# Twelve matrix products of zeros at the start of a hybrid decoder block on one core

## Chip, core and metric

The kernel runs on one NeuronCore of a Trainium2 chip. The metric is the device time of one execution in microseconds. The names of the engines are those of the profile: PE is TensorE (PEld its weight loads), DVE is VectorE, ACT is ScalarE, POOL is GpSimd and SP is SyncE, which issues most DMA transfers.

## The reference

The kernel computes one decoder block for a sequence of 1024 tokens of width 1024, all in float32: a gated recurrence of 8 heads beside a causal pooling mixer, then a squared-ReLU MLP of width 4096, each followed by a scaled residual and a layer norm.

```python
proj = x @ w_in                       # 1024 x 7168
q, f_pre, i_val, o_gate, pool_v, gate_a, gate_b = split(proj)
a = rms_norm_per_head(hgrn2(silu(q), 1 - f, i_val, log(f))) * g * sigmoid(o_gate) @ w_a
b = (causal_mean(pool_v) - pool_v) @ w_pool * pool_scale
mix = (sigmoid(gate_a) * a + sigmoid(gate_b) * b) @ w_out
x = layer_norm(alpha * x + mix)
x = layer_norm(alpha * x + square(relu(x @ w_up)) @ w_down)
```

## The kernel before

**Products.** A float32 matrix is split in two parts: ScalarE casts it to a rounded high part (L111 for weights, L116 for activations) and VectorE subtracts that from the source to get the low part (L112, L117). A product is then three matmuls (L188, L189, L190 in `prod`: high by high, high by low, low by high). The large products go through a seven-product Strassen scheme over halves of the tokens, the inner dimension and the columns. `pair` builds the steps for one pair of column blocks, `run` issues them, `w_blocks` loads four weight quarters, and the sums and differences of weight quarters are made on VectorE (L227, L262, L266).

**The start.** `prm_r` (lower bound logits, norm gain, pool scale) is loaded in three transfers from ScalarE's queue (L361 to L363), transposed on TensorE (L366), copied (L367), and made into `lb` and `one_lb` by VectorE and one exponential (L372 to L379). SyncE issues the loads of x in half rows (`load_x`, L386), mixed with loads of w_in quarters (L209): first the left half of token tiles 0 to 3 with the left quarters of the first block, then their right half with those of the second block, then token tiles 4 to 7, then the remaining quarters. Each tile of x is 128 tokens; `transposed_parts` (L147) turns four 128x128 squares of it into one PSUM bank and `split_into` makes the two parts, so that the tokens stand on the free axis. `first_tokens` does this for the quarters a11 and a12 of x (token tiles 0 to 3). `row_sums` then forms the Strassen sums of x on VectorE in place (L165 to L170), `second_tokens` transposes those, and `run_second` issues the remaining products.

**After that.** For each of the eight heads: products for its inputs, the recurrence in chunks (`hgrn`), and between them the pooling and gate products. Then the output products, the first layer norm, and the MLP with hidden blocks passed through DRAM.

**What sets the order.** The program is written once, and a scheduler that simulates a timeline orders the instructions of each engine (`schedule_with_timeline_sim`); on the chip each engine takes its instructions in that order. PSUM has eight banks: four of tag `pj`, two of `hg` and two of `tr`. The transposes of L147 take turns on the two `tr` banks, so a group of four waits until the group before the last has been read by VectorE's subtraction (L117). SBUF pools are filled from two sides; `const` holds the identity matrix for transposes, a mask and small constants.

Of the kernel before, what the change touches and what calls it, by code (L numbers as in the profile page):

```python
# [9 lines left out]
F32 = mybir.dt.float32  # L10
# [6 lines left out]
P = 128  # L17
# [12 lines left out]
PRIO_LAST = 3000  # L30
QUARTER = HALF // 2
PRIO = 60
WINDOWS = (2, 4, 8, 16)
ALPHA = 2.0 ** 0.25
LN_EPS = 1e-5
# [6 lines left out]
def tile_hybrid_block(  # L42
# [19 lines left out]
    V, A, G, PE = nc.vector, nc.scalar, nc.gpsimd, nc.tensor  # L62
# [5 lines left out]
    const = ctx.enter_context(tc.tile_pool(name="const", bufs=1))  # L68
# [10 lines left out]
    def nm(s):  # L79
        seq[0] += 1  # L80
        return f"{s}_{seq[0]}"
# [5 lines left out]
    def ps_tile(tag="pj", bufs=4):  # L87
        return pp.tile([P, HALF], F32, tag=tag, name=nm("ps_" + tag), bufs=bufs)
# [28 lines left out]
        V.tensor_sub(t[:, 1], src, f(t[:, 0]))  # L117


    ident = const.tile([P, P], F32, name="ident")  # L120
    make_identity(nc, ident)
    cmask = const.tile([P, P], F32, name="cmask")
# [61 lines left out]
    def prod(ps, w, name, first):  # L184
        wh, wl = w
        for k in range(CH):
            th, tl = xp[name][k][:, 0], xp[name][k][:, 1]
            PE.matmul(ps, wh[:, k], th, start=first and k == 0, stop=False, skip_group_check=True)  # L188
            PE.matmul(ps, wh[:, k], tl, start=False, stop=False, skip_group_check=True)  # L189
            PE.matmul(ps, wl[:, k], th, start=False, stop=k == CH - 1, skip_group_check=True)  # L190
# [51 lines left out]
    def pair(raw, rooms, takes, pz_tag="pj", twin=False):  # L242
# [5 lines left out]
        def copied(room, ps):  # L248
            t = room()
            A.copy(t, ps)  # L250
            return t

        def added(t, ps):
            V.tensor_add(t, t, ps)  # L254
            return t
# [25 lines left out]
        def p7(w):  # L281
            ps["z"] = ps_tile(pz_tag, 4 if pz_tag == "pj" else 2)
            prod(ps["z"], w, "s3", True)
            with tc.high_priority(PRIO):
                takes[0](added(c[11], ps["c"]))
                c[22] = copied(rooms[2], ps["z"])

        def p6(w):
            prod(ps["a"], w, "s2", False)
            with tc.high_priority(PRIO):  # L290
                c[21] = copied(rooms[1], ps["a"])

        def p4(w):
            prod(ps["z"], w, "a22", False)
            with tc.high_priority(PRIO):
                takes[2](added(c[21], ps["z"]))

        def p5(w):
            prod(ps["a"], w, "s1", False)
            with tc.high_priority(PRIO):  # L300
                takes[3](added(c[22], ps["a"]))

        def p3(w):
            prod(ps["a"], w, "s4", False)
            with tc.high_priority(PRIO):
                takes[1](ps["a"])
# [52 lines left out]
    with tc.tile_pool(name="xr", bufs=8, side="right", reuse_waits="tile") as xr:  # L359
# [5 lines left out]
        ps = ps_tile("tr", 2)  # L365
# [101 lines left out]
    with tc.tile_pool(name="tmp", bufs=1, side="right", reuse_waits="tile") as tmp:  # L467
# [79 lines left out]
        def pooled(g):  # L547

            j, win = 2 * g, WINDOWS[g]

# [239 lines left out]
    with tc.tile_pool(name="mg", bufs=1, side="right", reuse_waits="tile") as mg:  # L790
# [5 lines left out]
        for u in range(2):  # L796
            for jh in range(2):
# [8 lines left out]
                for g in (2 * jh, 2 * jh + 1):  # L806
# [6 lines left out]
                    for i in range(2):  # L813
                        w = slice(i * P, (i + 1) * P)
                        ps = ps_tile("hg", 2)
# [98 lines left out]
    with tc.tile_pool(name="up", bufs=1, side="right", reuse_waits="tile") as up:  # L914
# [85 lines left out]
        def add_to(t, n, ps):  # L1000
            y = r[t][:, n * HALF : (n + 1) * HALF]
            if (t, n) not in touched:
                V.scalar_tensor_tensor(y, y, ALPHA, ps, ALU.mult, ALU.add)
                touched.add((t, n))
            else:
                V.tensor_add(y, y, ps)
# [38 lines left out]
        def down_tile(ops, chain, fresh, c):  # L1045
            ps = banks[1 - chain][c]
            w = slice(c * P, (c + 1) * P)
            for n in range(M):
                hh, hl, wh, wl = (t[:, n % 2] for t in ops[n // 2])
                PE.matmul(ps, hh[:, w], wh, start=fresh and n == 0, stop=False, skip_group_check=True)  # L1050
                PE.matmul(ps, hh[:, w], wl, start=False, stop=False, skip_group_check=True)  # L1051
                PE.matmul(ps, hl[:, w], wh, start=False, stop=n == M - 1, skip_group_check=True)  # L1052
            return ps
# [74 lines left out]
    for i, c in ((0, 0), (0, 1), (1, 0), (0, 2), (1, 1), (1, 2), (0, 3), (1, 3)):  # L1128
        _, _, chain, fresh, (_, nh) = ends[i]
        ps = down_tile(ops[i], chain, fresh, c)  # L1130
        with tc.high_priority(PRIO) if c == CH - 1 else nullcontext():
            add_to(c, nh, ps)
# [36 lines left out]
```

## Time and profile before

| | us |
|---|---|
| median of three runs | 1501.65 |
| lowest and highest of them | 1501.17, 1505.73 |
| the profiled execution | 1503.59 |
| its span, first to last instruction | 1501.8 |
| PE busy | 1473.9 |
| DVE busy | 1117.6 |
| ACT busy | 743.4 |
| POOL busy | 53.5 |

The profiled execution is one more run, with the profiler on; its span leaves out 1.8 us around the instructions. Its instructions carry their start from the beginning of the span. A row of the timeline gives start, duration, engine, line, operation, result and sources, shapes and a count where equal neighbours are merged; in brackets stands how long the engine had been idle, and what ended it. TensorE's rows overlap, as its matmuls are pipelined; the distance of two starts is what one costs. The transposes of L147 and the product of L690 are float32 operations, those of L188 to L190 run on the rounded parts.

### The profile page before, as it was taken

To read this page: it belongs to the slowest core of one execution; us is meant where nothing else is said; L and a number is where in the kernel's file an instruction comes from. 1 tells how busy PE (TensorE), PEld (TensorE's weight loads), DVE (VectorE), ACT (ScalarE), POOL (GpSimd) and SP (SyncE) were. 2 spreads that over 40 slices of the span, in tenths; PEclk is the share of its full clock that TensorE was granted. 3 is DMA by queue.
4 is the path that set the end of the run, shared out by engine and by line. 5 is a ranking of instruction groups with operands and counts; after the bars stand their busy time and mean duration, and the time that the engine had idled before them with its cause. 6 is when DMAs were issued, how large, how long until landed. Compare 5 with 4: busy or idle time off the path is not lost.

```text
span 1501.8 us, 19944 instructions
## 1 busy us (share of the span) xinstructions
PE 1473.9 (98%) x7201; PEld 1222.7 (81%) x7201; DVE 1117.6 (74%) x1789; ACT 743.4 (49%) x1361; POOL 53.5 (4%) x244
## 2 busy tenths in 40 slices
PE   7999999999999999999999999999999999999997
PEld 5788888888888888888788877888888888888886
DVE  7778888989867777566766786666666787777977
ACT  4655555565564656554333245555555544333435
POOL 0000000000000000000001200000000100000000
PEclk9999999999999999999999999999999999999999
DMA  5112222222222122378654134444455783544422
GB/s 169 43 43 71 68 66 64 78 71 65 90 64 70 57 78 85 109 239 262 208 171 165 61 100 151 150 154 155 155 192 201 252 292 122 175 134 169 140 71 112
DMA packets 141825, 192.15 MB, mean 128 GB/s; under 512 B 9344, under 2 KB 80032, under 8 KB 141728
## 3 DMA queue, kind: packets, MB, share of 16 engines
q1 hardware_dynamic: 139792, 184.32, 37.1%
q0 software_dynamic: 1152, 4.19, 0.7%
q10 hardware_dynamic: 784, 2.38, 0.4%
q8 instruction: 56, 0.92, 0.3%
q14 instruction: 41, 0.34, 0.1%
HBM read 136.86 MB, written 54.00 MB: 127 GB/s over the span
## 4 chain that ended last, share of the span: by engine, by line
PE 91%; DVE 4%; DMA 3%; issue 1%; ACT 0%; SPq 0%; DVEq 0%; ACTq 0%
PE ps_pj L188 16%; PE ps_pj L190 16%; PE ps_pj L189 16%; PE ps_pj L1052 4%; PE ps_pj L1051 4%; PE ps_pj L1050 4%; PE ps_pj L461 3%; PE ps_hg L190 2%; PE ps_hg L189 2%; PE ps_hg L188 2%; PE ps_pj L99 2%; PE ps_pj L100 2%; PE ps_pj L98 2%; PE ps_hg L1052 1%; PE ps_hg L1051 1%; PE ps_hg L1050 1%
## 5 line engine op out<-in xcount | busy, mean ns | idle before, releaser
L189 PE MATMUL ps_pj<-act,w 128*128 128x512 f32 x1088 | 428.4, 394 | 0.7 <-DVE act L117 0.7
L188 PE MATMUL ps_pj<-act,w 128*128 128x512 f32 x1088 | 424.2, 395 | 1.9 <-ACT act L116 1.0
L190 PE MATMUL ps_pj<-act,w 128*128 128x512 f32 x1088 | 419.2, 392 | 0.4 <-DVE w L112 0.4
L188 PEld LDWEIGHTS ps_pj<-act,w 128*128 128x128 f32 x1088 | 204.4, 188 | 45.2 <-ACT w L111 2.4
L190 PEld LDWEIGHTS ps_pj<-act,w 128*128 128x128 f32 x1088 | 204.8, 188 | 42.9 <-DVE w L112 1.9
L189 PEld LDWEIGHTS ps_pj<-act,w 128*128 128x128 f32 x1088 | 204.9, 188 | 41.7 <-DVE act L117 1.2
L111 ACT CAST w<-t 128x512 fp32r<-128x512 f32 x176 | 108.6, 622 | 157.7 <-PE ps_pj L189 95.1
L112 DVE TENSOR_TENSOR w<-raw,w 128x512 fp32r<-128x512 f32 x161 | 110.3, 688 | 100.0 <-ACT w L111 83.0
L111 ACT CAST w<-raw 128x512 fp32r<-128x512 f32 x161 | 99.3, 620 | 115.3 <-PE ps_pj L189 50.9
L112 DVE TENSOR_TENSOR w<-t,w 128x512 fp32r<-128x512 f32 x176 | 120.3, 687 | 29.7 <-ACT w L111 22.5
L1012 ACT CAST act<-act 128x1024 fp32r<-128x1024 f32 x66 | 67.0, 1051 | 110.5 <-issue 35.0
L461 PE MATMUL ps_pj<-act,w 128*128 128x512 f32 x384 | 90.6, 394 | 2.9 <-DVE ga L822 2.9
L1013 DVE TENSOR_TENSOR act<-act,act 128x1024 fp32r<-128x1024 f32 x66 | 79.5, 1221 | 18.5 <-ACT act L1012 18.5
L254 DVE TENSOR_TENSOR c<-c,ps_pj 128x512 f32<-128x512 f32 x95 | 64.7, 682 | 38.0 <-PE ps_pj L190 31.9
L1052 PE MATMUL ps_pj<-act,act 128*128 128x512 f32 x240 | 92.9, 389 | 0.0
L1051 PE MATMUL ps_pj<-act,act 128*128 128x512 f32 x240 | 92.9, 389 | 0.0
L1050 PE MATMUL ps_pj<-act,act 128*128 128x512 f32 x240 | 92.5, 389 | 0.0
L461 PEld LDWEIGHTS ps_pj<-act,w 128*128 128x128 f32 x384 | 73.1, 191 | 18.7 <-DVE ga L822 3.3
L250 ACT COPY c<-ps_pj 128x512 f32<-128x512 f32 x95 | 55.1, 582 | 10.6 <-PE ps_pj L190 10.3
L189 PE MATMUL ps_hg<-act,w 128*128 128x512 f32 x144 | 57.0, 396 | 0.0
L190 PE MATMUL ps_hg<-act,w 128*128 128x512 f32 x144 | 56.2, 390 | 0.0
L188 PE MATMUL ps_hg<-act,w 128*128 128x512 f32 x144 | 55.2, 391 | 0.0
(312 smaller groups left out, 2522.2 us busy)
## 6 DMA issues: line engine op xcount, KB each, us to landing
h<-c SPq DMA_DIRECT2D x105, 256.0 KB, 2.7
raw<-in_w_in_dram SPq DMA_DIRECT2D x96, 256.0 KB, 3.4
act<-h SPq DMA_DIRECT2D x78, 256.0 KB, 3.0
draw<-in_w_down_dram SPq DMA_DIRECT2D x16, 1024.0 KB, 7.9
raw<-in_w_up_dram SPq DMA_DIRECT2D x30, 512.0 KB, 4.2
hf<-h SPq DMA_DIRECT2D x34, 256.0 KB, 3.0
raw<-in_w_a_dram SPq DMA_DIRECT2D x16, 512.0 KB, 5.2
xr<-in_x_dram SPq DMA_DIRECT2D x16, 256.0 KB, 5.6
```

The lines of the kernel that those rows point to most:

```text
L111: A.copy(hi, src)
L112: V.tensor_sub(lo, src, f(hi))
L188: PE.matmul(ps, wh[:, k], th, start=first and k == 0, stop=False, skip_group_check=True)
L189: PE.matmul(ps, wh[:, k], tl, start=False, stop=False, skip_group_check=True)
L190: PE.matmul(ps, wl[:, k], th, start=False, stop=k == CH - 1, skip_group_check=True)
L254: V.tensor_add(t, t, ps)
L461: PE.matmul(banks[j], a[:, w], b, start=k == 0 and i == 0, stop=k == KT - 1 and i == 2, skip_group_check=True,)
L1012: A.copy(hi, src)
L1013: V.tensor_sub(lo, src, f(hi))
L1050: PE.matmul(ps, hh[:, w], wh, start=fresh and n == 0, stop=False, skip_group_check=True)
L1051: PE.matmul(ps, hh[:, w], wl, start=False, stop=False, skip_group_check=True)
L1052: PE.matmul(ps, hl[:, w], wh, start=False, stop=n == M - 1, skip_group_check=True)
```

## The change

Ahead of the other constants, a 128x128 tile of zeros is made in `const` by VectorE, a `tr` bank of PSUM is taken, and twelve products of that tile with itself are written into its first 128 columns, one over the other. Nothing reads them. The constant `IDLE_PRODUCTS` sets their number. The lines of the kernel move down, those above it by one and those below it by seven (L111 becomes L112, L147 becomes L154), and the `tr` banks of all later transposes change places. The scheduler orders the changed program anew.

```diff
+IDLE_PRODUCTS = 12
...
+    zeros = const.tile([P, P], F32, name="zeros")
+    V.memset(zeros, 0.0)
+    ps = ps_tile("tr", 2)
+    for _ in range(IDLE_PRODUCTS):
+        PE.matmul(ps[:, :P], zeros, zeros, start=True, stop=True)
     ident = const.tile([P, P], F32, name="ident")
     make_identity(nc, ident)
```

## Prediction before the run

> **What bounds the kernel now.** I read the page first, then the chain that ended last in order of time, then the first 55 us of the timeline engine by engine, since the change adds work only there.
>
> ```profile
> span 1501.8 us, 19944 instructions
> PE 1473.9 (98%) x7201; PEld 1222.7 (81%) x7201; DVE 1117.6 (74%) x1789; ACT 743.4 (49%) x1361; POOL 53.5 (4%) x244
> ...
> PE 91%; DVE 4%; DMA 3%; issue 1%; ACT 0%; SPq 0%; DVEq 0%; ACTq 0%
> ```
>
> The kernel is bound by TensorE: 98% busy, 91% of the chain. What remains of the chain lies mostly at the start. In order of time it begins:
>
> ```profile
> 3.78 6.04 DMA xr<-in_x_dram
> 9.83 4.79 DMA xr<-in_x_dram
> 14.67 0.41 DVE c L165
> ...
> 33.38 0.61 DVE act L117
> 34.04 0.66 PE ps_tr L147 x4
> 34.69 0.23 PE ps_hg L189
> ```
>
> The reader is to see three legs: to 14.6 us the chain is the arrival of x, from 14.67 to 34.0 us it is VectorE, and TensorE carries it only from 34.04 us. So TensorE time won before 34 us counts only where it lets VectorE's row of work end sooner. The windows say the same (stretch, length, then busy time and count of PE, PEld, DVE, ACT, POOL, granted clock, DMA share, GB/s):
>
> ```profile
> 0.00:8.55 8.55, 2.47 (x9) 1.69 (x9) 1.31 (x8) 1.82 (x3) 1.75 (x27) 1.00 0.66 205
> 8.55:11.97 3.42, 2.54 (x7) 1.86 (x8) 1.89 (x3) 1.86 (x4) 0.00 (x0) 1.00 1.06 366
> 11.97:15.38 3.41, 3.41 (x11) 2.62 (x10) 2.62 (x5) 2.15 (x4) 0.00 (x0) 1.00 1.09 365
> 15.38:34.00 18.62, 15.43 (x83) 12.08 (x81) 18.62 (x32) 7.54 (x14) 0.00 (x0) 1.00 0.37 112
> 715.00:722.00 7.00, 4.15 (x12) 2.95 (x11) 6.72 (x11) 2.39 (x5) 0.00 (x0) 0.76 0.81 286
> ```
>
> VectorE is busy for all 18.62 us from 15.38 to 34.00, while before that it has gaps and DMA is full.
>
> **Is the clock low at the start?** The granted clock reads 1.00 there, but durations contradict it:
>
> ```profile
> 4.66 0.71 PE L147 MATMUL ps_tr<-ident,xr 128*128 128x128 f32 x2
> 6.83 1.54 PE L147 MATMUL ps_tr<-ident,xr 128*128 128x128 f32 x6 [1.46 <-DMA xr<-in_x_dram]
> 15.40 0.60 PE L147 MATMUL ps_tr<-ident,xr 128*128 128x128 f32 x4
> 19.97 1.03 PE L147 MATMUL ps_tr<-ident,xr 128*128 128x128 f32 x8
> ```
>
> Two transposes take 0.71 us and six 1.54, so one more costs 0.21; later four take 0.60 and eight 1.03, so one more costs 0.11. Up to about 15.4 us TensorE runs at half speed. The window 715 to 722 shows a granted 0.76: 0.24 of 7 us lost, which is one stretch of 3.4 us at half clock, costing 1.7 us.
>
> **The change, part by part.**
>
> 1. *The zeros.* One fill of 128x128 on VectorE. No row of before has it; the nearest are GpSimd's fill of the same shape and a small operation of VectorE:
>
> ```profile
> 0.86 0.20 POOL masks.py:197 MEMSET ident<- 128x128 f32 x1
> 5.92 0.20 DVE L377 RECIPROCAL lb<-lb 128x8 f32<-128x8 f32 x1
> ```
>
> I take 0.2 us. VectorE's first work of before needs the parameter transpose of 4.45 us, so the fill costs nothing (0.2 us without that cover). The 12 products can then begin at about 1.1 us.
>
> 2. *Twelve products.* Both operands are plain fp32. The kernel issues 64 such products at L690 (8 heads, 2 halves, 4 chunks) and the trace has 128 records, so each runs as two passes:
>
> ```profile
> L690 PE MATMUL ps_hg<-v,tH 128*128 128x128 f32 x128 | 16.8, 274 | 0.0
> ...
> 96.96 0.89 PE ps_hg L690 x8
> ```
>
> The first of these two lines is from the groups of TensorE by shape. Eight passes in 0.89 us is 0.11 each, as a transpose at full clock; at half clock I take a transpose's 0.21. Twelve products are 24 passes: 5.0 us at half clock, 2.7 at full. They end at 6.2 us at the latest, at 5.7 or so if the clock rises on the way. What is behind them on TensorE is the parameter transpose and the first two x transposes:
>
> ```profile
> 4.45 0.28 PE L366 MATMUL ps_tr<-ident,prm_r 32*128 32x32 f32 x1 [4.45 <-DMA prm_r<-in_pool_scale_dram]
> ...
> 8.22 0.62 ACT L111 CAST w<-raw 128x512 fp32r<-128x512 f32 x1 [2.54 <-DMA raw<-in_w_in_dram]
> 8.75 1.07 ACT L116 CAST act<-ps_tr 128x512 fp32r<-128x512 f32 x2
> 9.38 0.79 PE L188 MATMUL ps_pj<-act,w 128*128 128x512 f32 x1 [1.00 <-ACT act L116]
> ```
>
> These are late by up to 1.8 us, and that is covered: the third x tile lands only at 6.83, and ScalarE cannot copy a transposed tile before 8.75, because the weight cast ahead of it waits for its DMA until 8.22. Cost nothing; without that cover it would be up to 1.8 us.
>
> 3. *The clock.* In before, 2.54 of 3.42 us busy (8.55 to 11.97) did not raise it, 3.41 of 3.41 (11.97 to 15.38) did. Five us without a gap contain nearly all of such a stretch wherever it begins, so I expect full clock between 4.5 and 7 us. I then expect it to hold. Full clock speeds the transposes that VectorE waits for:
>
> ```profile
> 10.22 1.11 PE L147 MATMUL ps_tr<-ident,xr 128*128 128x128 f32 x4
> 11.37 0.59 ACT L116 CAST act<-ps_tr 128x512 fp32r<-128x512 f32 x1 [1.56 <-PE ps_tr L147]
> 11.99 0.69 DVE L117 TENSOR_TENSOR act<-ps_tr,act 128x512 fp32r<-128x512 f32 x1 [1.23 <-ACT act L116]
> 12.41 1.05 PE L147 MATMUL ps_tr<-ident,xr 128*128 128x128 f32 x4
> 12.80 1.14 ACT L111 CAST w<-raw 128x512 fp32r<-128x512 f32 x2 [0.84 <-DMA raw<-in_w_in_dram]
> 13.46 1.30 DVE L112 TENSOR_TENSOR w<-raw,w 128x512 fp32r<-128x512 f32 x2 [0.77 <-ACT w L111]
> 15.27 0.69 DVE L117 TENSOR_TENSOR act<-ps_tr,act 128x512 fp32r<-128x512 f32 x1
> ```
>
> VectorE idles 1.23 and 0.77 us here. With the four transposes in 0.60 instead of 1.11, the subtraction of 11.99 starts near 11.4; the next group of four, which stood at 12.41, comes behind three products at 0.23 and ends near 11.9; ScalarE is done near 12.5 and VectorE's subtraction of the fourth tile, which stood at 15.27, runs near 12.5, ahead of the weights at 13.46. L165 still starts at 14.67, when x lands, and VectorE's row behind it is one operation shorter: VectorE issues these 0.60 apart (14.67, 15.27). **Gain 0.6 us.**
>
> 4. *The order.* The scheduler lays the program out anew. The order of instructions as built differs from before in about the first 50 on VectorE, 30 on ScalarE and 160 on TensorE, and in a dozen about 890 us into the run; SyncE's 571, all loads of x and w_in among them, stand as before, and GpSimd's too. Three differences matter. The fourth tile's L117 is placed ahead of L165, which step 3 needs. The exponential of the parameters and four small VectorE operations (such as L377 above, 0.20 at most) move behind the first casts; with the 0.6 above this, 1.4 us in all, fits the 2.0 us of idling. And one L262 goes behind the subtraction that TensorE waits for at 34.04, so that wait ends one slot (0.6) sooner; the weight made from it comes 0.6 later than it could, but TensorE has other products first. **Between 0 and 0.6 more.** At 890 us four transposes change places with three products of 0.23, so at most 0.7 us of waiting could come or go; I take nothing.
>
> ```profile
> 32.69 0.69 DVE L262 TENSOR_TENSOR t<-t,raw 128x512 f32<-128x512 f32 x1
> 33.29 0.69 DVE L117 TENSOR_TENSOR act<-ps_tr,act 128x512 fp32r<-128x512 f32 x1
> ...
> 48.28 3.39 DMA raw<-in_w_in_dram
> ...
> 54.43 0.63 PE L147 MATMUL ps_tr<-ident,xr 128*128 128x128 f32 x4 [1.39 <-DVE act L117]
> ```
>
> What is late next is TensorE itself, from 34.04. Its wait at 54.43 goes back to the weight load of 48.28, which is released by casts that follow TensorE's own work, so it moves along.
>
> **Sum.** 0.6 + (0 to 0.6), and I take 0.9 us. The profiled execution took 1503.59 us (span 1501.8 and 1.8 around it), 1.94 above the median of the three runs, 1501.65. It would become 1502.7, and the median **1500.7 us**.
>
> **Rivals.**
>
> *The clock falls back (slower).* After the products TensorE has only transposes until 9.38. Two stretches of 3.41 us bear on what holds the clock:
>
> ```profile
> 30.44 0.66 PE L147 MATMUL ps_tr<-ident,xr 128*128 128x128 f32 x4 [1.38 <-DVE act L117]
> ...
> 29.03:32.44 3.41, 2.03 (x11) 1.60 (x11) 3.41 (x7) 1.66 (x3) 0.00 (x0) 1.00 0.00 0
> 715.11:718.52 3.41, 0.56 (x3) 0.13 (x3) 3.27 (x6) 1.67 (x4) 0.00 (x0) 1.00 0.94 327
> ```
>
> With 2.03 us busy, 0.66 of it transposes, it held; after 0.56 the half-clock stretch followed. In the changed kernel a stretch from 5.1 to 8.5 would hold about 0.6 us of products and 1.2 of transposes: 1.8 if both count, 0.6 if transposes do not. If it falls, the 10.22 to 13.46 work runs at the old pace, but the new order puts the fourth tile's cast (13.5, when the transposes of 12.41 end) ahead of the two weight casts of 12.80. These slip to 14.05, VectorE's L165 behind them to 15.8 instead of 14.67: 1.1 late less the 0.6 of the operation already done, **+0.5 us: 1502.2**. It decides from the point where the clock is lost before about 10.2 us. [...] No row of before separates the two, since in the stretch that held 1.4 us were products.
>
> *The gain does not arrive.* VectorE's idle time is filled by the moved small operations or by a cast that waits, and L165 waits for x as before: **1501.65**. For it speaks that x's arrival at 14.6 is untouched.
>
> *All of the half-clock time comes back.* PE's busy 2.47 + 2.54 + 3.41 = 8.4 us would halve, 4.2 us, at most **1497.4**; with the half-clock stretch of 718 us gone too (1.7), 1495.8. Against it speaks that VectorE, not TensorE, is full from 15.4 to 34.
>
> *More half-clock stretches later.* The waits near 54 and 716 us move against the gate's rhythm; each stretch costs 1.7, three **1506.7**.
>
> **How the numbers follow.** Forecast 0.50; clock falls back 0.20; no gain 0.13; all comes back 0.10; more stretches 0.07. A difference under 0.3% (4.5 us) is about what a measurement of this kernel can tell from no change. The first three lie within it: same 0.83, faster 0.10, slower 0.07. The range runs from 1497.4 (step 3's upper bound) to 1503.9 (clock falls back, and one more stretch: 1501.65 + 0.5 + 1.7) and leaves out the ends of the last two.
>
> **What would show it.** Right: zero products from about 1.1 to 5.7 us, whose spacing drops to 0.11; transposes at 10 us in 0.60; the fourth L117 before 13.5; L165 still at 14.67; TensorE's wait of 34.04 ending at 32.8 to 33.4. Wrong: transposes at 10 us still 1.1; L165 after 15; first casts later than 8.75; or a gap on TensorE past 50 us that before does not have.

## The result, and the profile after

| | before | after |
|---|---|---|
| median of 15 runs each, us | 1502.66 | 1506.68 |
| lowest and highest | 1500.74, 1505.73 | 1502.45, 1509.35 |
| the profiled execution | 1503.59 | 1507.91 |
| its span | 1501.8 | 1506.2 |

The ratio after to before is 1.0024, 95% interval 1.0016 to 1.0032: the kernel became slower by 4 us. The forecast was 1500.7, which is 0.95 below the 1501.65 that three runs of before had given; the range ended at 1503.9.

The page of the changed kernel, its span, busy times and chain by engine:

```profile
span 1506.2 us, 19995 instructions
PE 1478.9 (98%) x7225; PEld 1227.4 (81%) x7225; DVE 1117.7 (74%) x1790; ACT 743.2 (49%) x1361; POOL 53.3 (4%) x244
...
PE 90%; DMA 5%; DVE 4%; issue 1%; ACT 0%; SPq 0%; DVEq 0%; ACTq 0%
```

TensorE has 24 matmuls and 24 weight loads more and is 5.0 us longer busy. The chain's share of DMA rose from 3% to 5%, but this is a weak sign: most of the rise is the chain taking another path through x loads at the start and through transfers between 660 and 720 us, and the two loads that matter below make only 2.6 us of it.

The start in the timeline of the changed kernel:

```profile
0.91 0.17 DVE L123 MEMSET zeros<- 128x128 f32 x1 [0.91 <-PEq L1162]
...
1.13 4.99 PE L126 MATMUL ps_tr<-zeros 128*128 128x128 f32 x24 [1.13 <-DVE zeros L123]
...
8.53 0.62 ACT L112 CAST w<-raw 128x512 fp32r<-128x512 f32 x1 [5.07 <-DMA raw<-in_w_in_dram]
...
11.71 0.60 PE L154 MATMUL ps_tr<-ident,xr 128*128 128x128 f32 x4
...
12.96 0.69 DVE L118 TENSOR_TENSOR act<-ps_tr,act 128x512 fp32r<-128x512 f32 x1 [0.43 <-ACT act L117]
...
14.77 0.68 DVE L172 TENSOR_TENSOR c<-xr,xr 128x512 f32<-128x512 f32 x1
```

All of this is as forecast: the fill is free, the passes end near 6.1 us, four transposes take 0.60, the fourth tile's subtraction runs at 12.96 (12.5 was forecast), ahead of L172 (L165 of before) at 14.77. The first cast is 0.3 later, as its DMA landed later.

The loss stands behind TensorE's waits. From the timelines of TensorE, the changed kernel (in brackets the idle time), and then the kernel before:

```profile
32.94 1.11 PE L154 MATMUL ps_tr<-ident,xr 128*128 128x128 f32 x4 [1.58 <-DVE act L118]
...
56.08 0.63 PE L154 MATMUL ps_tr<-ident,xr 128*128 128x128 f32 x4 [2.63 <-DVE act L118]
...
178.48 0.71 PE L737 MATMUL ps_hg<-v,att 128*128 128x128 f32 x4 [1.91 <-DVE att L727]
...
724.06 4.40 PE L468 MATMUL ps_pj<-act,w 128*128 128x512 f32 x18 [2.28 <-DVE ga L829]
```

```profile
173.85 0.71 PE L730 MATMUL ps_hg<-v,att 128*128 128x128 f32 x4 [0.50 <-DVE att L720]
...
718.40 5.99 PE L461 MATMUL ps_pj<-act,w 128*128 128x512 f32 x18 [2.85 <-DVE ga L822]
```

And the changed kernel in the stretches before and behind three of these waits. A row gives the stretch, its length, busy time and count of PE, PEld, DVE, ACT and POOL, and then the granted clock, which is 1.00 or 0.50 here:

```profile
29.34:32.75 3.41, 1.62 (x6) 0.86 (x5) 3.41 (x6) 0.08 (x1) 0.00 (x0) 1.00 0.00 0
32.75:36.16 3.41, 3.22 (x10) 2.73 (x11) 3.41 (x7) 1.81 (x3) 0.00 (x0) 0.50 0.00 0
53.23:56.64 3.41, 0.78 (x6) 0.59 (x6) 3.20 (x6) 0.00 (x0) 0.00 (x0) 1.00 0.00 0
56.64:60.06 3.42, 3.42 (x12) 2.73 (x11) 1.19 (x2) 0.59 (x1) 0.00 (x0) 0.50 0.00 0
176.10:179.52 3.42, 1.51 (x11) 1.07 (x11) 3.28 (x7) 1.17 (x3) 0.00 (x0) 1.00 0.00 0
179.52:182.94 3.42, 3.42 (x14) 2.94 (x13) 2.66 (x5) 1.82 (x9) 0.49 (x3) 0.50 0.00 0
```

Lay the starts beside those of before. The wait of 34.04 ends at 32.94, 1.1 us sooner: the gain arrived. The next, 54.43, ends at 56.08: from 1.1 ahead to 1.65 behind, made of one half-clock stretch (1.7, half of 3.41) and a wait 1.24 longer (2.63 for 1.39). At 178.48 it is 4.63 behind: another stretch, and a wait 1.41 longer (1.91 for 0.50). At 724.06 it is 5.66 behind: the third stretch, less 0.57 of a shorter wait. Behind that, before has its stretch of 718.52 and after has none, so 4.4 remain at the end (1506.2 against 1501.8). **Two longer waits (2.65 us) and two more half-clock stretches (three against one, 3.4), less 1.1 won at the start and the 0.57: 4.4.** The sum agrees with the spans; it is an account of these two executions.

What do the two longer waits wait for? In the chain of waits in order of time, the loads ahead of them, in the changed kernel and then before (48.28 is in the prediction):

```profile
48.70 4.62 DMA raw<-in_w_in_dram
...
170.97 5.17 DMA raw<-in_w_in_dram
```

```profile
167.75 3.76 DMA raw<-in_w_in_dram
```

The same loads of 256 and 512 KB started 0.4 and 3.2 later and took 1.23 and 1.41 longer. TensorE itself came to the first of these waits only 0.41 later (53.45 for 53.04, the end of a wait less its length). So the longer load, not a late TensorE, is the longer wait. The view of DMA from 48 to 54 us (40 slices of 0.15 us) shows why, before and then after:

```profile
GB/s 0 0 0 0 0 3 82 75 92 119 249 328 348 335 348 345 348 345 266 157 51 3 0 0 0 0 0 0 0 0 0 0 0 0 0 0 0 0 0 0
...
q1 hardware_dynamic: 1056, 0.52, 30.0%
```

```profile
GB/s 0 0 0 0 0 0 0 0 14 82 109 82 123 263 321 352 345 430 324 331 283 205 143 65 31 10 7 14 7 17 20 24 3 0 0 0 0 0 0 0
...
q1 hardware_dynamic: 1056, 0.52, 30.5%
q8 instruction: 1, 0.02, 1.1%
```

Before, the load runs at some 345 GB/s and stops. After, one packet more lies in it, of the queue `q8 instruction`: 16 KB (the page of before counts 56 such packets, 0.92 MB), called a refill below, which starts at 50.65 and takes 1.0 us, and behind it some thirty of the load's 1056 packets trickle in at 7 to 24 GB/s for 1.2 us. In before the same refill comes at 55.7, as the view of 55 to 57 us says, behind the load:

```profile
DMA packets 1, 0.02 MB, mean 8 GB/s; under 512 B 0, under 2 KB 0, under 8 KB 0
...
q8 instruction: 1, 0.02, 3.3%
```

The second load has it too: the refill comes at 172.01 in before, 0.5 us behind the load's end (171.51), and at 173.79 in after, in the middle of the load (170.97 to 176.14). The view of 170.5 to 176.5 us of after, again in slices of 0.15 us, shows the load standing still for 0.6 us while the refill runs (173.79 to 174.91), and then the same trickle:

```profile
GB/s 0 0 0 0 0 0 0 0 0 0 109 82 96 143 225 287 382 382 375 410 355 485 144 62 14 0 0 0 0 7 14 7 14 7 7 0 0 0 0 0
```

Why a refill moves is seen by counting TensorE's instructions from the start up to it. In these rows the first two counts are PE's and PEld's; the two rows of before come first, then those of after:

```profile
0.00:55.71 55.71, 44.09 (x217) 34.66 (x218) 41.96 (x74) 25.03 (x45) 1.75 (x27) 1.00 0.42 133
0.00:172.01 172.01, 160.38 (x850) 132.20 (x851) 131.35 (x239) 90.00 (x178) 8.97 (x73) 1.00 0.27 83
...
0.00:50.65 50.65, 43.20 (x220) 34.88 (x221) 37.98 (x69) 22.74 (x41) 1.74 (x27) 0.97 0.45 141
0.00:173.79 173.79, 163.71 (x851) 135.53 (x852) 130.94 (x239) 89.61 (x176) 8.92 (x73) 0.98 0.26 82
```

Both refills come behind nearly the same number of TensorE's records in both kernels, 435 and 441, 1701 and 1703, and all the other kernels below have the first of the two behind 427 to 453. So I read the queue as the one that carries TensorE's code; 48 records more at the start, and each of these two refills came some 48 records earlier in the program. The first four runs below were made before this was seen, for another theory.

### The profile page after: what moved, and what is told of

The parts are those of the page before. It is cut to its first block, busy times and chain, and to the rows that moved or that the text cites. A ratio compares the mean times of both kernels' runs of the same rounds, so it can differ in the third digit from the quotient of the medians.

```text
span 1506.2 us, 19995 instructions
## 1 busy us (share of the span) xinstructions
PE 1478.9 (98%) x7225; PEld 1227.4 (81%) x7225; DVE 1117.7 (74%) x1790; ACT 743.2 (49%) x1361; POOL 53.3 (4%) x244
## 3 DMA queue, kind: packets, MB, share of 16 engines
q10 hardware_dynamic: 784, 2.38, 0.5%
## 4 chain that ended last, share of the span: by engine, by line
PE 90%; DMA 5%; DVE 4%; issue 1%; ACT 0%; SPq 0%; DVEq 0%; ACTq 0%
PE ps_pj L195 16%; PE ps_pj L196 15%; PE ps_pj L197 15%; PE ps_pj L1059 4%; PE ps_pj L1058 4%; PE ps_pj L1057 4%; PE ps_pj L468 3%; PE ps_hg L197 2%; PE ps_hg L196 2%; PE ps_hg L195 2%; PE ps_pj L101 2%; PE ps_pj L100 2%; PE ps_pj L99 2%; PE ps_hg L1059 1%; PE ps_hg L1058 1%; PE ps_hg L1057 1%
## 5 line engine op out<-in xcount | busy, mean ns | idle before, releaser
L112 ACT CAST w<-t 128x512 fp32r<-128x512 f32 x176 | 108.7, 622 | 154.2 <-PE ps_pj L196 95.1
L112 ACT CAST w<-raw 128x512 fp32r<-128x512 f32 x161 | 99.3, 620 | 112.0 <-PE ps_pj L196 51.6
L196 PE MATMUL ps_hg<-act,w 128*128 128x512 f32 x144 | 58.1, 403 | 0.0
L197 PE MATMUL ps_hg<-act,w 128*128 128x512 f32 x144 | 57.2, 397 | 0.4 <-DVE w L113 0.4
L195 PE MATMUL ps_hg<-act,w 128*128 128x512 f32 x144 | 56.2, 398 | 0.0
```

What stands on the lines that cost most here:

```text
L112: A.copy(hi, src)
```

## The experiments

**First theory (clock):** full clock early brings TensorE to its waits sooner, it idles longer in them, and drops to half clock. Rivals: the scheduler's new order; the bank exchange and the address shift that the zeros bring.

*e1_order_alone*: the new order, ten of the twelve products taken out of the finished program.

```diff
+    for b in nc.m.functions[0].blocks:
+        b.instructions = [
+            i for i in b.instructions
+            if not ("Matmult" in type(i).__name__ and i.ins[0].memref.startswith("zeros"))
+            or i.sync_info
+        ]
```

> The changed kernel with its new order of instructions, the fill and the exchange of the tr banks, but 10 of the 12 products taken out after scheduling (two remain, about 0.9 us). Clock theory (the early full clock lets TensorE reach its waits sooner, idle there longer and lose the clock again): TensorE starts at half clock as before, no half-clock stretch near 33, 57 and 180 us, time within 1.5 us of before (ratio 0.999 to 1.001). Order theory (the new order itself costs the time): about +4 us, as the change. The slower rival of the prediction: +0.5 us.

Measured: 1502.42 beside 1502.12, ratio 0.9998 (0.9988 to 1.0008). The order costs nothing that these runs can tell (0.08% at most).

*e2_warm_old_order*: the order of before, three products scheduled and nine more put behind them in the finished program.

```diff
-IDLE_PRODUCTS = 12
+IDLE_PRODUCTS = 3
+MORE_PRODUCTS = 9
```

> Twelve products as in the change, but scheduled with three of them, which leaves the order of every engine as before; the other nine are put in behind the first afterwards. Clock theory: full clock from about 5.5 us, then longer waits on TensorE before 57 us and one to three half-clock stretches of 3.4 us that before does not have: +2 to +5 us. Order theory: no loss, 0 to -0.6 us against before.

Measured: 1506.11, ratio 1.0023 (1.0011 to 1.0035). The loss is there without the new order.

*e3_fill_alone*: the fill and one product.

```diff
-IDLE_PRODUCTS = 12
+IDLE_PRODUCTS = 1
```

> The fill and one product (0.4 us): the order of before, the tr banks exchanged and the const pool 512 bytes larger. Clock theory and order theory: as before, within 1 us. A third theory, that the exchange of banks or of addresses costs the time: +4 us.

Measured: 1503.81, ratio 1.0006 (0.9998 to 1.0015). Banks and addresses cost 0 to 0.15%, not 0.24%.

*e5_hold*: the changed kernel, with 6, 9 and 6 products of zeros ("holds", which keep TensorE busy and change no result) added to a PSUM bank that is being accumulated, ahead of the waits of 32.9, 56.1 and 178.5 us.

```diff
+HELD = ((119, 6), (220, 9), (789, 6))
...
+        for _ in range(count):
+            nc.tensor.matmul(out, zero, zero, start=False, stop=False, skip_group_check=True)
```

> The changed kernel with 6, 9 and 6 more products of zeros, added without effect into banks that are being accumulated, put into TensorE's row ahead of its waits of 32.9, 56.1 and 178.5 us. Clock theory: the three half-clock stretches there go, 3 x 1.7 us: 1501 to 1503, that is 0 to -1.5 us against before. Order theory: the time stays near that of the change, +3.5 to +4.5 us, or gets worse by what the products take, up to 1 us.

Measured: 1501.67, ratio 0.9992 (0.9982 to 1.0002). I took this for proof of the clock theory. But e1 takes away the early clock and the products' code together, and the holds add code as well. The next four showed it.

*e9_again*: the changed kernel once more, one profile.

> The changed kernel once more, for a second trace. Clock theory: full clock again from 5 to 6 us, and at least one half-clock stretch of 3.4 us right behind one of the waits near 33, 56 and 178 us, at 1.7 us each; one execution between 1504 and 1509 us. Load theory (the early products lengthen the weight loads near 48 and 171 us and with them TensorE's waits at 56 and 178): in the five traces so far the load near 48 us took 3.4 us without early products (three kernels) and 4.2 to 4.9 with them (three kernels); it should take over 4 us again here. If that was chance, it is as likely to take 3.4.

Measured: 1504.61. The loads took 4.78 and 4.70, the waits 2.80 and 1.44, with refills at 50.91 and 173.79. The clock, though, fell back at 9.14 until 15.96, so TensorE was not early at 34 us (this wait ended at 34.57), and the loads were long all the same. This execution also shows the prediction's rival of the clock that falls back: L172 stands at 16.07 (15.8 given), and the wait ends 0.53 later than before's 34.04 (+0.5 given).

*e6_hold_first*: the hold of 32.9 us alone.

```diff
+HELD = ((119, 6),)
```

> The changed kernel with six products of zeros, added to an open PSUM bank, ahead of the wait of 32.9 us alone. Clock theory: the stretch near 33 us goes, worth at most 1.7 us, and the waits near 56 and 178 us still lose the clock in some executions: 1504 to 1506 us, mean granted clock between that of the changed kernel (0.9953) and that of the kernel with all three holds (0.9971). If the loss at 33 us causes the later ones by shifting them, all is given back: 1501.7. If the first one plays no part: 1506.7 as before this edit.

Measured: 1501.68, ratio 1.0001 (0.9991 to 1.0012), below my 1504 to 1506. One hold gave back as much as three. In its trace the wait near 54 us is as long (2.38) and the clock drops behind it; what is gone, beside the stretch near 33 us, is the long second load: it took 3.38, with the refill at 167.38, ahead of it. The six products of the hold are code too: 24 records, an estimated 2.7 us at the 9.0 per us that before shows from 24.36 to 55.71. The refill stands 6.4 ahead of after's 173.79, so the estimate gives less than half of it. The profiled execution was the slowest of the twelve, though (1505.97), so its trace does not show what the median execution did.

*e7_hold_old*: the three holds with one early product.

```diff
-IDLE_PRODUCTS = 12
+IDLE_PRODUCTS = 1
+HELD = ((108, 6), (209, 9), (778, 6))
```

> One early product only (so the clock rises late and the order is that of the kernel before) and the three holds of 6, 9 and 6 products ahead of the waits near 34, 54 and 173 us. Clock theory: at these waits the kernel before seldom loses the clock, so the holds bring at most a few tenths: 1501.5 to 1503, ratio to the kernel before 0.9990 to 1.0005; the five us that the holds gave in the changed kernel were those that the early products had cost. Rival, the holds help whatever stands ahead of them: 4 to 5 us here too, 1497.5 to 1499.

Measured: 1503.65, ratio 1.0016 (1.0007 to 1.0026), slower than either expected. The 42 passes of the holds are 4.6 us at 0.11, and the waits that they fill in this order were 1.12, 1.35 and 0.33 in e3_fill_alone: 1.8 too much.

*e8_transposes*: the kernel before with 24 transposes of the identity, and neither zeros nor products.

```diff
+IDLE_PRODUCTS = 24
...
+    ps = ps_tile("tr", 2)
+    for _ in range(IDLE_PRODUCTS):
+        PE.transpose(ps[:, :P], ident, ident)
```

> Instead of the twelve products, 24 transposes of the identity: as many passes of 128 columns on TensorE, all of them transposes. If transposes raise the clock as products do: full clock before 9 us, and the time of the changed kernel, 1504.5 to 1508. [...]

Measured: 1504.13, ratio 1.0016 (1.0005 to 1.0028), just under the 1504.5 to 1508 given for transposes that raise the clock. The windows of its trace:

```profile
1.66:6.65 4.99, 4.99 (x24) 4.98 (x24) 0.00 (x0) 1.28 (x1) 0.73 (x16) 1.00 0.84 260
6.65:10.06 3.41, 1.57 (x12) 1.10 (x10) 1.32 (x6) 1.19 (x3) 0.00 (x0) 1.00 1.00 341
10.06:13.47 3.41, 3.41 (x14) 2.51 (x13) 2.80 (x8) 1.93 (x4) 0.00 (x0) 0.50 1.11 346
```

Transposes alone raised the clock at 6.65 (four of them then take 0.66), and it fell at 10.06 after a stretch 46% busy. The load near 48 took 4.44, the one near 170 took 3.5.

**Second theory (code):** the early products' code moves TensorE's refills into the two loads. Two runs part it from the clock.

*e10_narrow*: order and count of after, but ten of the twelve products write 2 columns.

```diff
+COLUMNS = (2,) * 10
...
+    for columns in COLUMNS:
+        nc.tensor.matmul(out[:, :columns], zero, zero[:, :columns], start=True, stop=True)
```

> The changed kernel's order and its number of instructions, but 10 of the 12 early products write 2 columns instead of 128, so TensorE gets as much code and little work. Code theory (the 16 KB refill of TensorE's code, which comes at 55.7 us in the kernel before and at 50.65 in the changed one, falls into the weight load that starts at 48 us; the load takes 4.2 to 4.9 us instead of 3.4, and TensorE's wait behind it 2.4 to 2.9 instead of 1.4): refill between 49 and 51.5 us, load over 4 us, wait near 55 us over 2.2, and if this is what costs, 1504.5 to 1506.5. Clock theory (what costs is that the clock is full early, TensorE comes to its waits sooner and idles longer): clock full only at 12 to 15.4 us, and 1501.5 to 1503.

Measured: 1507.25 beside 1501.55, ratio 1.0030 (1.0018 to 1.0043), above my 1504.5 to 1506.5. **The whole loss without the early clock.** Its start, the waits and the loads (timeline and chain):

```profile
1.72 4.27 PE L1187 MATMUL ps_tr<-zeros 128*128 128x2 f32 x20
...
10.13 1.11 PE L155 MATMUL ps_tr<-ident,xr 128*128 128x128 f32 x4
...
57.60 0.63 PE L155 MATMUL ps_tr<-ident,xr 128*128 128x128 f32 x4 [2.76 <-DVE act L119]
```

```profile
50.09 4.75 DMA raw<-in_w_in_dram
...
172.51 4.66 DMA raw<-in_w_in_dram
```

The transposes of 10.13 still take 1.11; the clock is full from 14.12 only. Both loads are long, with refills at 52.17 and 174.78 inside them. (The refill missed the 49 to 51.5 that I gave, as the load was later too.)

*e11_wide*: the order of after and the same early work, 24 passes of 128 columns, in five products.

```diff
+SQUARES = (4, 4, 2)
...
+    for squares in SQUARES:
+        nc.tensor.matmul(bank[:, : squares * P], zero, zero.unsqueeze(1).to_broadcast([P, squares, P]), start=True, stop=True)
```

> The changed kernel's order and its early work, in 5 instructions instead of 12: two products of 128 columns, two of 512 and one of 256, 24 passes of 128 columns as before. Code theory: the refill comes near 53 to 54.5 us, behind the load of 48 us, which takes 3.4 us again; wait near 54 us about 1.4; 1501 to 1503. Clock theory: clock full from 5 to 7 us, stretches behind the waits near 33 and 54 us as in the changed kernel, 1505 to 1508. If both share the cost, 1503 to 1505.

Measured: 1501.04 beside 1501.55, ratio 0.9999 (0.9989 to 1.0008). **The early clock without the loss.** Its rows:

```profile
6.79 1.15 PE L155 MATMUL ps_tr<-ident,xr 128*128 128x128 f32 x8
...
55.83 0.63 PE L155 MATMUL ps_tr<-ident,xr 128*128 128x128 f32 x4 [1.34 <-DVE act L119]
```

```profile
49.73 3.34 DMA raw<-in_w_in_dram
```

Eight transposes in 1.15 at 6.79 say full clock; the load takes 3.34, the refill comes at 56.88, and the wait is 1.34. The clock theory had 1505 to 1508 here and falls. The clock even dropped twice in this trace, at 10.20 and from 30.68 to 37.51, and the median does not show it. So the clock was early here but did not stay; e12_wide_hold, next, has it full from 4.78 to 878.59 and no loss either. The trace of e10_narrow has half clock from 31.19 to 38.01 as well, so this stretch is not what parts the two kernels.

*e12_wide_hold*: that, and a hold of 12 passes in two instructions at 32.9 us.

```diff
+    for squares in (4, 2):
+        nc.tensor.matmul(held[:, : squares * P], ..., start=False, stop=False, skip_group_check=True)
```

> As e11_wide, and 12 passes of zeros in two instructions (512 and 256 columns) added to the open PSUM bank ahead of the wait of 32.9 us. If code and the wait at 33 us each bear a part of the loss, both are mended here: clock full from 6 us through the waits at 33 and 54 us, 1499.5 to 1501.5, below the kernel before. If the hold costs as much as it saves, it stands with e11_wide.

Measured: 1500.28, ratio 0.9996 (0.9986 to 1.0005): the lowest median, not told apart from before or e11_wide.

All traces side by side (us; "in" where the refill starts inside the load; the first three columns are of the profiled execution alone, the ratio is that of all runs):

| kernel | refill, load near 48 | refill, load near 170 | this execution | ratio |
|---|---|---|---|---|
| before | 55.71, 3.39 | 172.01, 3.76 | 1503.59 | 1 |
| e1_order_alone | 54.94, 3.39 | 171.48, 3.73 | 1500.43 | 0.9998 |
| e3_fill_alone | 55.04, 3.36 | 171.65, 3.58 | 1502.13 | 1.0006 |
| e11_wide | 56.88, 3.34 | 172.79, 3.5 | 1502.77 | 0.9999 |
| e12_wide_hold | 49.65 in, 3.37 | 169.45 in, 3.5 | 1499.43 | 0.9996 |
| e7_hold_old | 51.24 in, 3.4 | 167.62, 3.7 | 1503.34 | 1.0016 |
| e5_hold | 47.50 in, 4.20 | 162.26, 3.5 | 1502.71 | 0.9992 |
| e6_hold_first | 47.22 in, 4.36 | 167.38, 3.38 | 1505.97 | 1.0001 |
| e8_transposes | 50.43 in, 4.44 | 172.00 in, 3.5 | 1504.57 | 1.0016 |
| e2_warm_old_order | 51.53 in, 4.91 | 174.39 in, 3.87 | 1509.51 | 1.0023 |
| after | 50.65 in, 4.62 | 173.79 in, 5.17 | 1507.91 | 1.0024 |
| e9_again (after) | 50.91 in, 4.78 | 173.79 in, 4.70 | 1504.61 | one run |
| e10_narrow | 52.17 in, 4.75 | 174.78 in, 4.66 | 1510.12 | 1.0030 |

No load is long without a refill in it. Execution by execution, the six traces without a long load took 1499.43 to 1503.59 us, the four with the first alone long 1502.71 (where a hold fills the wait) to 1509.51, and the three with both long 1504.61 to 1510.12. By all runs, with both loads long the ratio is 1.0024 and 1.0030. With the first alone long it is 1.0001 (e6), 1.0016 (e8) and 1.0023 (e2, whose trace also has a half-clock stretch of 6.8 us from 721), and 0.9992 where a hold fills the wait (e5). With none it is 0.9996 to 1.0006, and 1.0016 where holds outlast their waits (e7). Not every refill inside a load hurts: both of e12_wide_hold, the second of e8 and the first of e7 did nothing, the second of e2 at most 0.5. In e12 the first starts 0.65 before the load lands, and the last packet of the load ends at 49.90, before the refill does. All five start so late, at most some 0.25 us before the load's last packet ends. But the first refill of e2, at 51.53, came when the load was all but done, and seven packets of it moved only behind the refill, from about 52.5 on, so that the load took 4.91. Why these packets moved only behind the refill, while those five loads lost little or nothing, no trace here shows.

## Why the prediction was wrong

1. *The zeros*: right, 0.17 us and free.
2. *Twelve products*: the time was right (4.99 at half clock, to 6.1 us against 5.7), the cover held. **"Cost nothing" is the step that failed.** I counted what the products keep TensorE busy with, and not what their instructions take: 48 more records of TensorE's code; the refills of 55.71 and 172.01 came about 48 records earlier in the program. The rows for an estimate were in the trace of before:

```profile
24.36:55.71 31.35, 26.68 (x141) 20.84 (x140) 27.16 (x45) 15.71 (x29) 0.00 (x0) 1.00 0.12 34
```

From one refill of `q8` (24.36) to the next (55.71) TensorE takes 281 records in 31.35 us, 9.0 per us. 48 more are 5.4 us: an estimated refill at 50.3, inside the load of 48.28 to 51.67 that the prediction quoted. Measured: 50.65. That it comes so close is in part luck, as the records between two refills vary (241 in the next 24.50 us of before). TensorE itself shows no wait at this refill: its rows of after have no idle time from 50.10 to 52.84. The load beside it took 4.62 for 3.39.
3. *The clock*: it rose at 5.44, inside 4.5 to 7, and held until 32.75 in the profiled execution, where "I then expect it to hold" ended: the stretch of half clock from there to 36.16 costs 1.7, more than the 1.1 won. In e9_again it fell back at 9.14, as the rival of 0.20 had it. The gain at the start was right: L172 at 14.77, TensorE's wait of 34.04 ends at 32.94 (I gave 32.8 to 33.4).
4. *The order*: right that it is worth little (e1: 0.9998). Wrong: "Its wait at 54.43 goes back to the weight load of 48.28 … so it moves along". The load's start moved along with TensorE, which the stretch at 33 us had by then put behind (48.70 for 48.28); its length was taken as given, and it grew from 3.39 to 4.62.

Of the rivals, *more half-clock stretches later* came near (three of them; 1506.7 given, 1506.68 measured), but that the numbers meet is luck: before has a stretch that after has not, so two net, and 2.65 us of the loss are waits that this rival did not have. Nor is a shift against the clock's rhythm the cause that the runs show. There is a rhythm in both traces: the changes of after at 5.44, 32.75, 56.64 and 179.52 lie 8, 7 and 36 steps of 3.413 us apart, those of before at 15.38 and 718.52 lie 206. But two of the three stretches stand behind waits that grew by 1.2 to 1.4 us and left 3.41 us only 23 and 44% busy, and near 54 us five of the six traces with such a longer wait have one behind it (not e8), and none of the seven with a wait of up to 1.39 or a hold in it. So the 4 us are two waits and the two stretches behind them. The stretch at 33 us (47% busy) has no refill near (those of after stand at 21.27 and 50.65) and is put down to the clock alone, and the one at 718 us that before has and after has not offsets it; why the latter is gone is open. In e11 too the clock dropped again, from 30.68 to 37.51, and in e9 already at 9.14, so what it wins at the start it may lose again. The other rivals fall: no gain (0.13) and all comes back (0.10) do not give a slower kernel. Where the clock fell back (e9_again), +0.5 us is seen at the wait of 34.04, but not in the time of the whole. Whether transposes count, which that rival left open, e8_transposes shows in part: 24 of them, without a product, raised the clock at 6.65.

**What stays open.** Why the refill does not move in proportion: with 1, 2 and 5 early products (e3, e1, e11) it stands 1.03 to 1.05 behind the end of the wait near 54 us (1.28 in before), with 12 ahead of it; five products should have moved it by 2.2 (20 records at 9.0 per us; I expected a refill at 53 to 54.5), and against that wait it moved by 0.2. The count of records at that refill, 427 to 453, is no sharper than that. And how often each stretch occurs: an execution without a profile shows only a mean clock, 0.9953 over the runs of after and 0.9975 over those of before beside e1. The difference is 3.3 us of clock time in 1502, about two stretches; but e11_wide has 0.9958 and no loss, so the mean alone does not say which stretches cost time.

## What to carry to other kernels

Instructions added to a busy engine cost code as well as time (here 48 records more brought a refill from 55.71 to 50.65): find the engine's `instruction` packets in the DMA view, count the engine's records up to each, and see into which load a packet moves when the new records are added to the count. A load that the chain runs through is the one to compare first when a change far from it costs time, and its length is not a constant (3.34 to 4.91 us here for the load near 48). An experiment that takes work away takes its code away too; to part the two, keep the number of instructions and change their size (e10_narrow), then the other way round (e11_wide).

## What the runs showed of the hardware

- Fifteen loads of 0.52 MB had one 16 KB code packet of about 1.0 us (0.93 to 1.41) inside. Ten of them took 0.8 to 1.5 us longer than those of before.
- The clock fell after stretches of 3.41 us that were 47, 23 and 44% busy (and 46% in e8_transposes), with waits of 1.58, 2.63 and 1.91 us in them, and held after one of 60% in before. The busy share alone does not decide it: in e9_again it fell after 63% (5.72 to 9.14), in e1_order_alone it held after 1.52 us of 3.41, 44% (875.90 to 879.31).
- A float32 pass of 2 columns costs as much as one of 128 at half clock (4.27 us for 20, 4.99 for 24: 0.21 each), and TensorE reads as busy, for 3.41 of 3.41 us from 3.88 to 7.29 in e10_narrow (such passes to 5.84, then full ones and transposes), but the clock did not rise by it: full only from 14.12, against 5.44 in after and 15.38 in before.
